# Operand sets of the down products: low parts written into the loaded tiles, loads and splits on other product numbers

## The chip, the cores and the metric

One core of a Trainium2 chip runs the whole program. The metric is device time in microseconds from launch to end, as the median of several runs. TensorE (PE) multiplies, VectorE (DVE) and ScalarE (ACT) work on tiles in the on-chip memory, GpSimd (POOL) and SyncE (SP) here mostly issue transfers (DMA).

## The reference, cut to what matters

Two layers of a hybrid encoder on 1024 positions of width 1024. Each layer ends in a gated feed-forward network of width 2816, which is where the change lies:

```python
for layer in range(DEPTH):
    ...
    hn2 = rmsnorm(h, norm2_g[layer])
    ff = jax.nn.silu(hn2 @ ffn_w_gate[layer]) * (hn2 @ ffn_w_up[layer])
    h = h + ff @ ffn_w_down[layer]
return rmsnorm(h, final_g)
```

All of it is float32.

## The kernel before

**Numbers in two parts.** Every operand of a matmul is split: a high part, cast by ACT to a rounded format (`...h`, `whi`, `whs`), and a low part, what is left, subtracted by DVE (`...l`, `wlo`, `wls`). A product of a 128 x 128 weight block and a 128 x 512 tile then takes three matmuls: high by high, high by low, low by high (L192, L193, L194 in `piece`).

**Quads.** Large parts of the feed-forward network are computed by a scheme of seven products in place of eight for a 2 x 2 block matrix. For it weights and activations are combined by additions first. A *gate quad* (`quad_items`) computes gate and up of one feature tile f from the normed activations (`rf`, `tt0` to `tt3`); a *down quad* (`down_quad`) computes two output tiles from a *chunk* of features. A product accumulates into the PSUM banks x, y, v and w (tiles `qx`, `qy`, `qv`, `qw`). The order of the seven is x with b11, y with t1, v with t0, x with b21, y with t2, w with t3, v with b22. Between them small operations run: `first` copies bank x into `qp` on ACT (L1325 in the down quads), `second` adds bank y to it as `qu` on DVE (L1329), `third` makes `qc` from y and v. In gate quads the results go through a tanh (`ts`, L1408 and L1425), then `half0` and `half1` (L1417 to L1430) form the feature tiles.

**Chunks.** Layer 0 has two chunks of down quads, of 8 and 6 features; layer 1 has three, of 8, 8 and 6. Four down quads belong to a chunk (two to the last one of a layer), so there are five *begins*, at which a new chunk's operands are needed for the first time. The first begin of a layer follows on the last gate quad. A product of a chunk of 8 features has 4 tiles and 12 matmuls, of one of 6 features 3 tiles and 9 matmuls.

**Operand sets.** When a feature pair is done, `keep` and `row` (L1215 to L1218, tiles `ft`) write the four blocks (b..) and the four combinations (t0 to t3) to DRAM (`fd`). At a begin the seven sets (`SETS`) come back: `op_load` issues one load per tile on SP's queue (L1225, into `fr`), `op_split` casts and subtracts (helper `split`, L115 and L116, into `foh` and `fol`). All these tiles, and most others of 128 x 512, come from one pool of 86 slots; an allocation waits until a slot is free.

**What sets the order.** The program is a list of items, one for each product with the small operations between. The table in `more` hangs loads and splits on product numbers: before the change set k of seven is loaded at product t0 - 12 + k * 17 // 10 and split at t0 - 4 + k, where t0 is the begin's number. (An eighth set, b12, of a layer's last chunk is loaded and split at numbers of its own, which stay.) A scheduler then puts the instructions of the list into an order for each engine, by priority in the list and by the time it believes operands and slots to be ready, so the order on an engine is not that of the list. Each engine works through its order strictly in sequence.

Weights come through SP's queue into four buffers (`raw`, L124), are combined (`sm`, `s`, L143 to L150) and split (L157 on ACT, L158 on DVE).

Of the kernel before, what the change touches and what calls it, by code (L numbers as in the profile page):

```python
# [8 lines left out]
F32 = mybir.dt.float32  # L9
F32R = mybir.dt.float32r  # L10
# [3 lines left out]
ADD, SUB, MUL = ALU.add, ALU.subtract, ALU.mult  # L14
# [13 lines left out]
QUAD_FROM = (8, 3)  # L28
DOWN_QUADS = 2
SETS = ("b11", "t1", "t0", "b21", "t2", "t3", "b22")  # L30
QUAD_LOOK = 5
NEG = -1e30
EPS = 1e-6
# [65 lines left out]
class Trunk:  # L99
# [99 lines left out]
    def emit(self):  # L199
# [11 lines left out]
        for i, (fn, gs) in enumerate(self.seq):  # L211
# [12 lines left out]
            if gs:  # L224
                n = max(pos[id(g)] for g in gs) + 1
                if isinstance(gs[0], QuadPart):
                    if self.split_ < min(len(order), n + QUAD_LOOK):
                        held = sum(last[id(g)] > i and not g.slots for g in order[:self.split_])
# [949 lines left out]
    def ffn_items(self, l, fill, head):  # L1178
# [3 lines left out]
        nc, V = self.nc, self.nc.vector  # L1182
        ff = [{}, {}]
        quads = QUAD_FROM[l]
        groups, chunks = GROUPS[l], CHUNKS[l]
# [4 lines left out]
        act, fd, ops = {}, {}, {}  # L1190
# [29 lines left out]
                put(c, f"t{k}", j, t)  # L1220

        def op_load(c, kind):
            ts = ops[c, kind] = [self.A("fr") for _ in range(chunks[c][1] // 2)]
            for j, t in enumerate(ts):
                nc.sync.dma_start(t, fd[c, kind, j])  # L1225

        def op_split(c, kind):
            ops[c, kind] = [self.split(t, "fo") for t in ops[c, kind]]

        def gate(f, h, g, st, part=None):  # L1230
            if part != 1:
# [225 lines left out]
        for i, (G, go, U, uo) in enumerate(blocks):  # L1457
            if i == 0:

                G1, go1, U1, uo1 = blocks[1]  # L1460
                a, b, c = (self.halves(x) for x in head[-3:])
# [27 lines left out]
        def at(t, fn):  # L1489
            more.setdefault(t, []).append((fn,))  # L1490

        for t0, c in begins:
            for k, kind in enumerate(SETS):
                at(t0 - 12 + k * 17 // 10, lambda c=c, kind=kind: op_load(c, kind))
                at(t0 - 4 + k, lambda c=c, kind=kind: op_split(c, kind))
        c = len(chunks) - 1
        end = 7 * len(made)

# [8 lines left out]
        at(end - 7 * DOWN_QUADS - 1, start_last)  # L1507
        at(end - 7 * DOWN_QUADS - 1, lambda: residual(H_AHEAD))
        at(end - 8, lambda: op_load(c, "b12"))
        at(end - 3, lambda: op_split(c, "b12"))  # L1510
        t = 0

# [25 lines left out]
        if fill:  # L1538
            a = len(head) + 12
            b = fill_end  # L1540
# [265 lines left out]
```

## Time and profile before

| | us |
|---|---|
| median of 3 runs | 2648.95 |
| lowest and highest | 2644.98, 2649.7 |
| the profiled execution's own time | 2647.83 |
| its span, first to last instruction | 2646.1 |
| TensorE busy in it | 2564.8 |

The 1.7 us between the profiled time and its span lie outside the instructions. Shares of busy time are means over stages with different limits: TensorE is busy almost always, so what counts is where it stands still, and which instruction ends that. The granted clock tells how fast TensorE ran in a stretch: 1.00 is 2.4 GHz, 0.50 is 1.2 GHz, values between are a mixture over time.

### The profile page before, as it was taken

How to read it: one execution, taken by the hardware profiler on the slowest of the kernel's cores; microseconds unless marked ns; L12 is line 12 of the kernel's file. 1: busy time of each engine (PE TensorE's matmuls, PEld its weight loads, DVE VectorE, ACT ScalarE, POOL GpSimd, SP SyncE). 2: the span in 40 equal slices, each digit the busy share in tenths (PEclk: the TensorE clock that was granted, in tenths of full speed). 3: DMA queues.
4: the chain of work that ended last, by engine and by line, in shares of the span. 5: the costliest groups of instructions: out<-in, count | busy, mean ns of one | idle time of the engine just before them, and what ended most of it. 6: DMA issues, size and time to landing. Idle time of an engine off the chain costs nothing.

```text
span 2646.1 us, 35134 instructions
## 1 busy us (share of the span) xinstructions
PE 2564.8 (97%) x12722; PEld 2088.1 (79%) x12722; DVE 1827.9 (69%) x3577; ACT 1022.1 (39%) x1949; POOL 321.3 (12%) x528
## 2 busy tenths in 40 slices
PE   8999899999999999998999999999999999998997
PEld 6787677887888888886787778888878888886776
DVE  9986878575977677677763465756377777676766
ACT  5336744422443333233444553453233222234432
POOL 0141011000142111011100001200001011111110
PEclk9999999999999999998999999999999999998998
DMA  3453435354174533255732244434322233255773
GB/s 139 136 186 118 136 120 180 124 186 140 55 197 132 98 110 108 96 202 137 200 133 76 72 140 161 159 120 167 127 92 93 102 104 116 92 199 156 176 190 123
DMA packets 160510, 357.01 MB, mean 135 GB/s; under 512 B 22048, under 2 KB 44832, under 8 KB 160336
## 3 DMA queue, kind: packets, MB, share of 16 engines
q1 hardware_dynamic: 117136, 236.28, 26.9%
q0 software_dynamic: 43200, 118.48, 15.9%
q8 instruction: 100, 1.64, 0.2%
q14 instruction: 74, 0.61, 0.1%
HBM read 230.97 MB, written 123.68 MB: 134 GB/s over the span
## 4 chain that ended last, share of the span: by engine, by line
PE 88%; DVE 7%; ACT 2%; issue 1%; DMA 1%; SPq 0%; DVEq 0%; ACTq 0%
PE pj L181 6%; PE pj L182 6%; PE pj L183 6%; PE qx L192 3%; PE qx L193 3%; PE qx L194 3%; PE qy L192 3%; PE qy L194 3%; PE qy L193 3%; PE qv L192 3%; PE qv L193 3%; PE qv L194 3%; PE wo L181 2%; PE wo L183 2%; PE wo L182 2%; PE br L181 2%
## 5 line engine op out<-in xcount | busy, mean ns | idle before, releaser
L181 PE MATMUL pj<-rah,whi 128*128 128x512 f32 x768 | 306.2, 399 | 0.4 <-DVE sm L804 0.4
L182 PE MATMUL pj<-ral,whi 128*128 128x512 f32 x768 | 300.1, 391 | 0.7 <-DVE ral L116 0.7
L183 PE MATMUL pj<-rah,wlo 128*128 128x512 f32 x768 | 299.9, 391 | 0.0
L170 DVE TENSOR_TENSOR wlo<-raw,whi 128x1024 fp32r<-128x1024 f32 (+1 forms) x126 | 145.7, 1156 | 168.3 <-ACT whi L169 159.0
L169 ACT CAST whi<-raw 128x1024 fp32r<-128x1024 f32 (+1 forms) x126 | 125.3, 995 | 273.9 <-PE pj L182 115.1
L181 PEld LDWEIGHTS pj<-rah,whi 128*128 128x128 f32 x768 | 144.7, 188 | 35.4 <-issue 4.7
L182 PEld LDWEIGHTS pj<-ral,whi 128*128 128x128 f32 x768 | 144.8, 189 | 30.9 <-DVE ral L116 2.6
L183 PEld LDWEIGHTS pj<-rah,wlo 128*128 128x128 f32 x768 | 144.5, 188 | 30.8
L1425 ACT ACTIVATE ts<-qu 128x512 f32<-128x512 f32 x33 | 20.9, 633 | 287.2 <-DVE qu L1423 287.2
L804 DVE CUSTOM_DVE_ANT_0 x<-s,bias,nsink 128x384 f32<-128x384 f32 (+1 forms) x128 | 67.5, 581 | 64.0 <-PE s L798 63.9
L1423 DVE TENSOR_TENSOR qu<-qu,qv 128x512 f32<-128x512 f32 x33 | 22.7, 687 | 125.8 <-PE qv L194 125.8
L192 PE MATMUL qx<-rfh,whi 128*128 128x512 f32 x264 | 102.7, 389 | 0.0
L193 PE MATMUL qx<-rfl,whi 128*128 128x512 f32 x264 | 102.7, 389 | 0.0
L194 PE MATMUL qx<-rfh,wlo 128*128 128x512 f32 x264 | 102.7, 389 | 0.0
L976 ACT COPY s5sg<-s5s 64x256 f32<-64x256 f32 x128 | 51.7, 404 | 128.8 <-DVE s5s L971 127.4
L181 PE MATMUL wo<-mgh,whi 128*128 128x512 f32 x256 | 100.0, 391 | 0.0
L1196 POOL DMA_DIRECT2D fd_b<-ts x60 | 32.6, 543 | 553.4 <-DVE ts L1419 464.2
L183 PE MATMUL wo<-mgh,wlo 128*128 128x512 f32 x256 | 99.7, 389 | 0.0
L182 PE MATMUL wo<-mgl,whi 128*128 128x512 f32 x256 | 99.6, 389 | 0.0
L157 ACT CAST whs<-s 128x512 fp32r<-128x512 f32 (+1 forms) x98 | 59.9, 612 | 99.3 <-DVE s L150 93.3
L157 ACT CAST whi<-sm 128x1024 fp32r<-128x1024 f32 (+1 forms) x49 | 50.6, 1033 | 122.7 <-PE qv L193 102.9
L158 DVE TENSOR_TENSOR wlo<-sm,whi 128x1024 fp32r<-128x1024 f32 (+1 forms) x49 | 58.9, 1202 | 41.8 <-ACT whi L157 41.7
(468 smaller groups left out, 7191.0 us busy)
## 6 DMA issues: line engine op xcount, KB each, us to landing
raw<-in_w_in SPq DMA_DIRECT2D x52, 512.0 KB
raw<-in_w_gate SPq DMA_DIRECT2D x44, 512.0 KB
raw<-in_w_up SPq DMA_DIRECT2D x44, 512.0 KB
fd_t<-ft POOLq DMA_DIRECT2D x72, 256.0 KB, 2.7
fr<-fd_t SPq DMA_DIRECT2D x72, 256.0 KB
g<-th POOLq DMA_DIRECT2D x64, 256.0 KB, 2.8
thr<-g SPq DMA_DIRECT2D x64, 256.0 KB
fd_b<-ts POOLq DMA_DIRECT2D x60, 256.0 KB, 2.3
```

The source lines that it names most:

```text
L157: nc.scalar.copy(g.hi[:, n], src)
L158: V.tensor_tensor(g.lo[:, n], src, g.hi[:, n].bitcast(F32), SUB)
L169: nc.scalar.copy(g.hi[:, :n], g.raw[:, :n])
L170: nc.vector.tensor_tensor(g.lo[:, :n], g.raw[:, :n], g.hi[:, :n].bitcast(F32), SUB)
L181: mm(ps, lhsT=wh, rhs=xh, start=k == 0, stop=False)
L182: mm(ps, lhsT=wh, rhs=xl, start=False, stop=False)
L183: mm(ps, lhsT=wl, rhs=xh, start=False, stop=k == n - 1)
L192: mm(ps, lhsT=wh, rhs=xh, start=start and k == 0, stop=False)
L193: mm(ps, lhsT=wh, rhs=xl, start=False, stop=False)
L194: mm(ps, lhsT=wl, rhs=xh, start=False, stop=k == len(xs) - 1)
L804: V.tensor_tensor_reduce(out=x[:, :n], in0=ps[:, :n], in1=self.bias[hd][:, bo:bo + n], op0=ADD, op1=ALU.min, scale=-1.0, scalar=self.nsink ...
L976: nc.scalar.copy(SG[64 * r:64 * r + 64, g * 256:(g + 1) * 256].rearrange("p (d n) -> p d n", d=2), Sv[64 * g:64 * g + 64, :, r])
```

## The change

The low part of a set is written into the tile that was loaded, so that a tile of a set holds two slots (loaded tile and high part) instead of three while it is split. And the product numbers of loads and splits are read from two tables, `LOADS` and `SPLITS`. Against the begin the loads of the seven sets move from -12, -11, -9, -7, -6, -4, -2 to -14, -10, -8, -7, -5, -4, -2, the splits from -4, -3, -2, -1, 0, 1, 2 to -10, -6, -4, -2, 0, 2, 3.

```diff
 SETS = ("b11", "t1", "t0", "b21", "t2", "t3", "b22")
+
+LOADS = (-14, -10, -8, -7, -5, -4, -2)
+SPLITS = (-10, -6, -4, -2, 0, 2, 3)
...
         def op_load(c, kind):
-            ts = ops[c, kind] = [self.A("fr") for _ in range(chunks[c][1] // 2)]
+            ts = ops[c, kind] = [self.A("fol", F32R) for _ in range(chunks[c][1] // 2)]
             for j, t in enumerate(ts):
-                nc.sync.dma_start(t, fd[c, kind, j])
+                nc.sync.dma_start(t.bitcast(F32), fd[c, kind, j])
 
         def op_split(c, kind):
-            ops[c, kind] = [self.split(t, "fo") for t in ops[c, kind]]
+
+            pairs = []
+            for lo in ops[c, kind]:
+                hi = self.A("foh", F32R)
+                nc.scalar.copy(hi, lo.bitcast(F32))
+                V.tensor_tensor(lo, lo.bitcast(F32), hi.bitcast(F32), SUB)
+                pairs.append((hi, lo))
+            ops[c, kind] = pairs
...
         for t0, c in begins:
-            for k, kind in enumerate(SETS):
-                at(t0 - 12 + k * 17 // 10, lambda c=c, kind=kind: op_load(c, kind))
-                at(t0 - 4 + k, lambda c=c, kind=kind: op_split(c, kind))
+            for kind, a, b in zip(SETS, LOADS, SPLITS):
+                at(t0 + a, lambda c=c, kind=kind: op_load(c, kind))
+                at(t0 + b, lambda c=c, kind=kind: op_split(c, kind))
```

The diff also moves line numbers: cast and subtraction of these sets are L1235 and L1236 in the changed kernel, the loads L1228, and lines behind them stand 10 further down (`first` L1335, `second` L1339), those ahead 3.

The number of instructions on each engine stays the same; their order does not. On DVE round the first begin of layer 0, before (`wlo` is the low part of the next down quad's combined weights, `qc` a sum of the last gate quad, `fol` low parts of the sets):

```order
L116 TENSOR_TENSOR fol<-fr,foh 128x512 x4
L1417 SCALAR_TENSOR_TENSOR ts<-ts,qx 128x512
L158 TENSOR_TENSOR wls<-raw,whs 128x512
L116 TENSOR_TENSOR fol<-fr,foh 128x512 x4
L158 TENSOR_TENSOR wlo<-sm,whi 128x1024
L1413 TENSOR_TENSOR qc<-qp,qv 128x512
L116 TENSOR_TENSOR fol<-fr,foh 128x512
L1418 TENSOR_TENSOR qp<-qp,qw 128x512
```

and now:

```order
L1427 SCALAR_TENSOR_TENSOR ts<-ts,qx 128x512
L161 TENSOR_TENSOR wls<-raw,whs 128x512
L1236 TENSOR_TENSOR fol<-fol,foh 128x512 x4
L1423 TENSOR_TENSOR qc<-qp,qv 128x512
L161 TENSOR_TENSOR wls<-s_11108,whs 128x512
L1428 TENSOR_TENSOR qp<-qp,qw 128x512
L1236 TENSOR_TENSOR fol<-fol,foh 128x512
L1429 SCALAR_TENSOR_TENSOR ts<-qp,ts 128x512
L1236 TENSOR_TENSOR fol<-fol,foh 128x512 x3
L1433 TENSOR_TENSOR qu<-qu,qv 128x512
L161 TENSOR_TENSOR wlo<-sm,whi 128x1024
```

`wlo`, which stood ahead of the gate's `qc`, stands behind `qc` and behind `qu`; the four `fol` of b21, which stood among the gate's sums, are all ahead of `qc`, and those of t2 ahead of `qu`.

A few instructions on, still DVE at that begin, before (the `ts` and `ft` are the last gate quad's `half1` and `row`; the first four `fol` are t2's, the second four t3's):

```order
L116 TENSOR_TENSOR fol<-fr,foh 128x512 x4
L1215 TENSOR_TENSOR ft<-ts 128x512
L1429 SCALAR_TENSOR_TENSOR ts<-ts,qu 128x512
L1430 SCALAR_TENSOR_TENSOR ts<-qc,ts 128x512
L1216 TENSOR_TENSOR ft<-ts,ft 128x512
L1217 TENSOR_TENSOR ft<-ts 128x512
L1218 TENSOR_TENSOR ft<-ts,ft 128x512
L116 TENSOR_TENSOR fol<-fr,foh 128x512 x4
L146 TENSOR_TENSOR s_11360<-raw,sm 128x512
```

and now (the first four `fol` are t3's, the last four b22's; `qu` is the first down quad's `second`):

```order
L1439 SCALAR_TENSOR_TENSOR ts<-ts,qu 128x512
L1218 TENSOR_TENSOR ft<-ts 128x512
L1440 SCALAR_TENSOR_TENSOR ts<-qc,ts 128x512
L1219 TENSOR_TENSOR ft<-ts,ft 128x512
L1220 TENSOR_TENSOR ft<-ts 128x512
L1221 TENSOR_TENSOR ft<-ts,ft 128x512
L149 TENSOR_TENSOR s_11324<-raw,sm 128x512
L1236 TENSOR_TENSOR fol<-fol,foh 128x512 x4
L1339 TENSOR_TENSOR qu<-qp,qy 128x512
L1236 TENSOR_TENSOR fol<-fol,foh 128x512 x4
```

t3's four still follow on `half1` and `row`; `second`, which stood further down behind b22's, stands between t3's and b22's.

On ACT round the second begin of layer 0 (`whi` from `sm` is the high part of combined weights, `qp` the copy of `first`), before; the first three `foh` are t1's, the next six t0's and b21's, the six behind `whi` t2's and t3's, the last three b22's:

```order
L115 CAST foh<-fr 128x512 x3
L1336 COPY dx<-qx 128x512
L157 CAST whs<-raw 128x384
L115 CAST foh<-fr 128x512 x6
L157 CAST whi<-sm 128x768
L157 CAST whs<-s_11808 128x384
L115 CAST foh<-fr 128x512 x6
L1325 COPY qp<-qx 128x512
L115 CAST foh<-fr 128x512 x3
```

and now (b21's, t2's, t3's and, behind `whi`, b22's):

```order
L1235 CAST foh<-fol 128x512 x3
L160 CAST whs<-s_11792 128x384
L1235 CAST foh<-fol 128x512 x3
L1335 COPY qp<-qx 128x512
L1235 CAST foh<-fol 128x512 x3
L160 CAST whi<-sm 128x768
L1235 CAST foh<-fol 128x512 x3
```

The casts of t2 and t3 and the copy, which stood behind `whi`, stand ahead of it.

## Rows read from the trace of the kernel before

**Rows 1.** The page, busy us (share of the span) xinstructions of each engine
```profile
PE 2564.8 (97%) x12722; PEld 2088.1 (79%) x12722; DVE 1827.9 (69%) x3577; ACT 1022.1 (39%) x1949; POOL 321.3 (12%) x528
```

**Rows 2.** Waits of PE: line, waited for: us in total, times, longest us
```profile
PE qw L193 <- DVE fol L116: 14.8, 5, 6.3
PE qw L192 <- ACT foh L115: 13.5, 5, 3.2
...
PE qv L192 <- DVE qc L1413: 5.5, 2, 2.8
```

**Rows 3.** Windows: stretch, its us, PE busy (xmatmuls), granted clock, DMA share, GB/s
```profile
1140.00:1200.00 60.00, 60.00 (x266) 1.00 0.56 194
1190.00:1250.00 60.00, 48.99 (x199) 0.89 0.47 122
1285.00:1315.00 30.00, 26.19 (x102) 0.89 0.74 203
...
2470.00:2510.00 40.00, 35.92 (x151) 0.96 0.64 134
2557.00:2587.00 30.00, 26.19 (x103) 0.89 0.65 186
```

**Rows 4.** Timeline of PE, layer 0's first begin: start, us, line, op [idle before]
```profile
1205.37 0.78 PE L192 MATMUL qv<-rfh,whs 128*128 128x512 f32 x1 [2.77 <-DVE qc L1413]
1205.95 0.63 PE L193 MATMUL qv<-rfl,whs 128*128 128x512 f32 x1
1206.38 0.63 PE L194 MATMUL qv<-rfh,wls 128*128 128x512 f32 x1
...
1218.84 0.79 PE L193 MATMUL qw<-fol,whs 128*128 128x512 f32 x1 [6.24 <-DVE fol L116]
```

**Rows 5.** Timeline of DVE at the same begin
```profile
1203.49 1.22 DVE L158 TENSOR_TENSOR wlo<-sm,whi 128x1024 fp32r<-128x1024 f32 x1 [2.29 <-ACT whi L157]
1204.63 0.68 DVE L1413 TENSOR_TENSOR qc<-qp,qv 128x512 f32<-128x512 f32 x1
...
1210.03 0.69 DVE L1423 TENSOR_TENSOR qu<-qu,qv 128x512 f32<-128x512 f32 x1 [1.71 <-PE qv L194]
...
1214.24 0.69 DVE L1215 TENSOR_TENSOR ft<-ts 128x512 f32<-128x512 f32 x1
...
1218.10 2.49 DVE L116 TENSOR_TENSOR fol<-fr,foh 128x512 fp32r<-128x512 f32 x4
```

**Rows 6.** Timeline of ACT, at layer 0's first begin and at its second
```profile
1210.81 0.63 ACT L1425 ACTIVATE ts<-qu 128x512 f32<-128x512 f32 x1 [2.66 <-DVE qu L1423]
...
1294.59 0.83 ACT L157 CAST whi<-sm 128x768 fp32r<-128x768 f32 x1 [7.87 <-issue]
...
1295.74 3.21 ACT L115 CAST foh<-fr 128x512 fp32r<-128x512 f32 x6
```

**Rows 7.** Timeline of PE, second begins of layer 0 and of layer 1
```profile
1297.96 0.80 PE L192 MATMUL qw<-foh,whs 128*128 128x512 f32 x1 [3.23 <-ACT foh L115]
1299.34 0.79 PE L193 MATMUL qw<-fol,whs 128*128 128x512 f32 x1 [0.58 <-DVE fol L116]
...
2487.39 0.50 PE L192 MATMUL qw<-foh,whs 128*128 128x512 f32 x1 [2.99 <-ACT foh L115]
2488.97 0.79 PE L193 MATMUL qw<-fol,whs 128*128 128x512 f32 x1 [1.09 <-DVE fol L116]
```

**Rows 8.** Two lines of DVE: op xcount, ns min/median/max, first and last start
```profile
L116 DVE TENSOR_TENSOR fol<-fr,foh x132: 681/686/693, 1185.0 to 2589.3; 128x512 fp32r<-128x512 f32 x132
...
L144 DVE TENSOR_TENSOR sm<-sm,raw x49: 557/691/698, 909.2 to 2550.3; 128x512 f32<-128x512 f32 x45, 128x384 f32<-128x384 f32 x4
```

**Rows 9.** Timeline of PE, a short idle in layer 0's gates
```profile
675.54 0.50 PE L181 MATMUL fg<-rfh,whi 128*128 128x512 f32 x1 [1.69 <-ACT rfh L115]
675.88 0.40 PE L181 MATMUL fu<-rfh,whi 128*128 128x512 f32 x1
```

**Rows 10.** Waits of SP's queue, 1140 to 1300
```profile
SPq L124 <- DVE s L150: 76.5, 6, 24.9
```

## The prediction

> **What bounds the kernel now.** I read the page's busy row first, then TensorE's waits, then its timeline at the places they name, then DVE's and ACT's timelines at the same places. TensorE is busy 2564.8 us, 97% of the span [rows 1], so a change in the operands' preparation is worth at most the time for which TensorE stands still on them, and what its clock loses after. The waits list names three such entries that belong to the chunk begins: on the low part `fol` 14.8 us, on the high part `foh` 13.5, on the gate's sum `qc` 5.5, together 33.8 us [rows 2]. The other entries of the list belong to code that the diff leaves alone.
>
> Idle time is not the whole loss. Behind a stall matmuls start 0.43 us apart (1205.95 to 1206.38), against 60 / 266 = 0.2256 us in an undisturbed stretch at granted clock 1.00 [rows 3, 4]. So I count the matmuls that are missing in a stretch round each begin [rows 3]. The first begin of layer 0 (1190 to 1250): 266 - 199 = 67, times 0.2256 = 15.1 us; layer 1's first begin has the same 199. The second begin of layer 0: 133 - 102 = 31, or 7.0 us. Layer 1's second: 177.3 - 151 = 26.3, or 5.9 us. Layer 1's third: 133 - 103 = 30, or 6.8 us. The sum, 2 x 15.1 + 7.0 + 5.9 + 6.8 = **49.9 us, is the ceiling** of what the change can bring: 33.8 idle and some 16 of slow clock.
>
> The Trainium skill, "TensorE: Matmul & The Clock Gate", section "Back-to-back issue gap", gives 512 / 2.4 + 2.5 = 216 ns for a warm matmul of 512 columns. By that pitch the ceiling would be an estimated 47.7 us. The trace's 0.2256 stays in the sum.
>
> **What happens at a begin.** Two patterns. (a) First begins. On DVE `wlo` stands ahead of `qc` and waits until 1203.49 for ACT, so `qc` comes at 1204.63 and the gate's seventh product starts 2.77 us late. Then DVE is full from 1210.03: `qu`, low parts of b21 and t2, the gate's six last sums (`half1` and `row`) from 1214.24 to 1218.10, and only then the four `fol` of t3, for which TensorE has been idle 6.24 us by 1218.84 [rows 4, 5]. (b) The other three begins. On ACT the cast `whi` takes a buffer that t0's product has to free first; it starts at 1294.59 after 7.87 us of idle, with the casts of t2 and t3 queued behind it. These run from 1295.74, and TensorE stands 3.23 + 0.58 us [rows 6, 7].
>
> **Part 1: low parts in the loaded tiles.** Nothing is added to an engine: one cast and one subtraction per tile as before, 132 of each. A subtraction in place costs what another does: `sm<-sm,raw` 691 ns, `fol<-fr,foh` 686 [rows 8]. The price is 0 +/- 132 x 0.005 us = 0.7 us of DVE time, hidden under TensorE either way. An operand tile holds two slots instead of three while it is split, so casts wait less for slots. I put that at 0 by itself; its effect is in the new order.
>
> **Part 2: loads and splits spread.** The same loads and splits, five begins of seven sets with three or four tiles each, move by up to six products of 12 x 0.2256 = 2.7 us (9 x 0.2256 = 2.0 us in the three-tile chunk).
>
> *`qc` at the first begins.* In the new order `wlo` stands behind `qc` and `qu`. In front of `qc` are the four subtractions of b21 instead (four take 2.49 us at 1218.10, so 0.60 apart). Counting DVE from the start s of the chunk's first product (s = 1194.28 in the trace), `qc` ends at about s + 5.9, and the gate's seventh product, now after eleven matmuls of t0, wants it at s + 7.9. The 2.77 us stall goes, with 2 us to spare.
>
> *t3 at the first begins.* Here the split of t3 still stands behind the gate's last sums: in the new order qu, wlo, ts, ft, ts, ft, ft, ft, s4, then t3's four. Moving t2 and b21 ahead has emptied the queue before `qu`, but not behind it. And a new wait is added: the sum `qu` of `second` (L1339) stands behind those four, and product t2 overwrites the bank that it reads. The chain from the end of the gate's seventh product (s + 10.8): `qu` 0.60, `wlo` 1.14 (its pitch from 1203.49 to 1204.63), six sums 3.86 (1214.24 to 1218.10), s4 0.60, four `fol` 2.4, `qu` 0.69 [rows 5] = 9.3; with 0.15 us of hand-over t2 starts at s + 20.25. Without stalls it would start at s + 13.6. So 6.65 us are still lost. Part of it shows as another new wait: b21's product waits for the copy of `first`, which stands on ACT behind the tanh (1210.81, 0.63 us, 0.78 after `qu`) [rows 6]: 0.60 + 0.18 + 0.63 after the seventh product's end and about 0.5 for the copy; that is 1.7 us of the 6.65, since only one matmul lies between. Behind both waits are queued, on TensorE, all matmuls of t2, t3 and b22, ready or not.
>
> The Trainium skill, "TensorE: Matmul & The Clock Gate", section "Step-by-step: what each phase is for", states that matmuls stay in program order and only weight loads are pulled ahead. The trace shows it: in the 6.24 us ahead of 1218.84 TensorE starts no matmul of any product [rows 4]. If it could step past a blocked product these 6.65 us would mostly vanish; that is rival A's time.
>
> On the clock: at layer 1's second begin 2.99 + 1.09 = 4.08 us of idle cost 5.9 in all, so 1.8 for the clock; at layer 0's second 3.81 idle cost 7.0, so 3.2 [rows 3, 7]. After 1.69 us of idle at 675.54 the next matmul came 0.34 us later, at no lasting drop [rows 9]. Of the new idle (1.7 and 4.9 us) only the second should drop the clock: I take 1.8, the shorter price, because the engine is busy on both sides of the short one. So a first begin loses 6.65 + 1.8 = 8.4 instead of 15.1: **6.7 us gained at each, 13.4 for two**; with 3.2 it is 10.6.
>
> *The other three begins.* In the new order t2's three casts and the copy stand ahead of `whi` on ACT (all of t3's too in the three-tile chunk of layer 0's second and layer 1's third begin; two of t3's four behind it in layer 1's second). TensorE no longer waits for them: t3's parts are there 3 us early. What comes last next is `qu` of `second` again: `whi` 0.83 [rows 6], `wlo` 1.14 x 768 / 1024 = 0.86, `qu` 0.69 after t0's product ends = 2.4 us, against twelve matmuls of b21 and t3 in between, 12 x 0.2256 = 2.7 us. The slack is **0.3 us** there, about 0.45 at layer 1's second. I take these stalls as gone: 7.0 + 5.9 + 6.8 = **19.7 us**.
>
> *Loads.* b11's loads go to SyncE's queue two products earlier, those of t1, t0 and t2 one later, and the splits move up: the lead from load to split, 8, 8, 7, 6, 6, 5, 4 products in the order of the sets, becomes 4, 4, 4, 5, 5, 6, 5. Its least, four products or 10.8 us, was there before for b22, and no wait on a load stands in TensorE's list. SyncE's own waits are on weights' buffers, up to 24.9 us [rows 10]; the loads' places among those are almost as before, so I put it at 0.
>
> **Sum.** 13.4 + 19.7 = 33.1 us. Profiled execution 2647.83 - 33.1 = 2614.7. The median lies 1.1 higher: **2615.8**, say 2616.
>
> **Rivals.** *A, all goes:* the last sums of the gate get out of t3's way and nothing replaces them: 2648.95 - 49.9 = 2599. For it: all splits start earlier. Against it: t3's stand behind the same sums, and the waits are the same kind. *B, the thin slacks fail:* 0.3 us is a fraction of one DVE operation (0.60), and if one comes in between at the three later begins, a stall of one to three us with its clock takes most of the 19.7: only 13.4 is left, 2635.5. *C, the change doesn't do what it says at the first begins:* the earlier splits only shift DVE's backlog, and 15.1 stays at both: 2648.95 - 19.7 = 2629. *D, slower: late loads.* Place: SyncE's queue ahead of a begin, where loads follow a weight load that waits (24.9 us at worst [rows 10]). With the lead cut to 10.8 us for three sets a late load holds ACT and DVE, which take their work in order, and with them the gates' `qc`. Price: each us late passes on, plus 1.8 us of clock. At five begins it turns the sign from 33.1 / 5 - 1.8 = 4.8 us late at each; 10 us late at each gives 2615.8 + 5 x 11.8 = 2675. Against it: b22 lived with that lead before.
>
> **Chances.** Forecast (2606 to 2626, with partial failures) 0.58; A 0.08; B 0.17; C 0.07; D 0.10, half of it deep enough to be slower, half to land within 0.2% (5.3 us, about what a measurement of this kernel can tell from no change). Faster 0.90, same 0.05, slower 0.05. Range 2600 to 2638: from just above A past B, leaving out A and D.
>
> **What would show it.** In the profile after: no wait of the seventh product on `qc`; at the two first begins one idle of about 1.7 us before qx ended by the copy or tanh, and one near 5 us before qy ended by `qu`; at the three others no wait over 0.5 us; 227 to 232 matmuls in the 60 us round a first begin; the three entries' 33.8 us of idle down to about 13, and the other entries as before. Wrong it would be made by waits on `foh` or `fol` behind a load, or by a wait of qy t2 at the later begins.

## The result, and the profile after

The changed kernel takes **2614.23 us** (median of 4 runs, 2614.16 to 2614.47) against 2649.32 for the kernel before, run beside it (2644.98 to 2650.9). The ratio is 0.987, 95% interval 0.9853 to 0.9887: some 35 us gained. The profiled execution's span fell from 2646.1 to 2612.7.

TensorE's waits of the changed kernel (line, waited for: us in total, times, longest us). The first and the last are all that is left at the begins; the one between them belongs to the program's start.

```profile
PE qy L195 <- DVE qu L1339: 8.6, 2, 4.3
PE pj L184 <- ACT xgh L372: 7.0, 1, 7.0
...
PE qx L195 <- ACT qp L1335: 3.4, 2, 1.7
```

The three entries of [rows 2] on `fol`, `foh` and `qc`, 33.8 us, are gone. Two new ones of 12.0 us stand there, each twice: once at the first begin of each layer. Windows of the same kernel (stretch, its us, PE busy (xmatmuls), granted clock, DMA share, GB/s):

```profile
1190.00:1250.00 60.00, 54.00 (x230) 0.97 0.57 140
...
1260.00:1300.00 40.00, 40.00 (x178) 1.00 0.86 242
2360.00:2420.00 60.00, 54.00 (x227) 0.94 0.58 158
2440.00:2490.00 50.00, 50.00 (x222) 1.00 0.78 190
2530.00:2570.00 40.00, 40.00 (x178) 1.00 0.62 183
```

At the first begins 36 and 39 matmuls are missing, 8.1 and 8.8 us by the 0.2256 us apart, where 67 were [rows 3]. At layer 0's second begin (1260 to 1300) and layer 1's second and third (2440 to 2490, 2530 to 2570) none is. So 49.9 us of loss became 16.9: 33.0 us, which is the fall of the span but for 0.4.

TensorE at layer 0's first begin, after (start, us, line, op, idle before):

```profile
1194.13 0.39 PE L195 MATMUL qx<-foh,whi 128*128 128x512 f32 x1
...
1206.86 0.50 PE L195 MATMUL qx<-foh,whi 128*128 128x512 f32 x1 [1.69 <-ACT qp L1335]
1207.20 0.39 PE L196 MATMUL qx<-fol,whi 128*128 128x512 f32 x1
...
1214.20 0.71 PE L195 MATMUL qy<-foh,whs 128*128 128x512 f32 x1 [4.31 <-DVE qu L1339]
1214.71 0.63 PE L196 MATMUL qy<-fol,whs 128*128 128x512 f32 x1
1215.14 0.63 PE L197 MATMUL qy<-foh,wls 128*128 128x512 f32 x1
...
1217.95 0.39 PE L195 MATMUL qy<-foh,whs 128*128 128x512 f32 x1
```

b21's product waits 1.69 us for the copy of `first`, t2's product 4.31 us for the sum of `second`; only behind the second wait are matmuls 0.43 us apart. DVE in that time:

```profile
1199.48 0.69 DVE L1423 TENSOR_TENSOR qc<-qp,qv 128x512 f32<-128x512 f32 x1
...
1204.98 0.69 DVE L1433 TENSOR_TENSOR qu<-qu,qv 128x512 f32<-128x512 f32 x1 [0.60 <-PE qv L197]
1205.59 1.22 DVE L161 TENSOR_TENSOR wlo<-sm,whi 128x1024 fp32r<-128x1024 f32 x1
1206.72 0.68 DVE L1439 SCALAR_TENSOR_TENSOR ts<-ts,qu 128x512 f32<-128x512 f32 x1
...
1210.46 0.68 DVE L149 TENSOR_TENSOR s<-raw,sm 128x512 f32<-128x512 f32 x1
1211.06 2.49 DVE L1236 TENSOR_TENSOR fol<-fol,foh 128x512 fp32r<-128x512 f32 x4
1213.47 0.68 DVE L1339 TENSOR_TENSOR qu<-qp,qy 128x512 f32<-128x512 f32 x1
```

`qc` comes at 1199.48, where before it stood behind `wlo` [rows 5]. From the gate's `qu` at 1204.98 on DVE does not pause until `second`'s `qu` ends at 1214.15, and TensorE goes on 0.05 us later.

### The profile page after: what moved, and what is told of

Read it like the earlier page. It is cut to its first block, busy times and chain, and to the rows that moved or that the text cites. A ratio compares the mean times of both kernels' runs of the same rounds, so it can differ in the third digit from the quotient of the medians.

```text
span 2612.7 us, 35123 instructions
## 1 busy us (share of the span) xinstructions
PE 2550.7 (98%) x12722; PEld 2079.1 (80%) x12722; DVE 1826.8 (70%) x3577; ACT 1022.5 (39%) x1949; POOL 322.5 (12%) x528
## 4 chain that ended last, share of the span: by engine, by line
PE 88%; DVE 8%; ACT 2%; issue 1%; DMA 1%; SPq 0%; DVEq 0%; ACTq 0%
PE pj L184 6%; PE pj L185 6%; PE pj L186 6%; PE qy L195 3%; PE qy L196 3%; PE qy L197 3%; PE qv L195 3%; PE qv L196 3%; PE qv L197 3%; PE qx L195 3%; PE qx L197 3%; PE qx L196 3%; PE wo L184 2%; PE wo L186 2%; PE wo L185 2%; PE br L184 2%
## 5 line engine op out<-in xcount | busy, mean ns | idle before, releaser
L1236 DVE TENSOR_TENSOR fol<-fol,foh 128x512 fp32r<-128x512 f32 x132 | 83.3, 686 | 0.2 <-ACT foh L1235 0.2
```

The source lines that it names most:

```text
L1236: V.tensor_tensor(lo, lo.bitcast(F32), hi.bitcast(F32), SUB)
```

## The experiments

**The two halves of the change, each alone.** The first experiment (e1) keeps the in-place low parts and puts the old numbers back:

```diff
-LOADS = (-14, -10, -8, -7, -5, -4, -2)
-SPLITS = (-10, -6, -4, -2, 0, 2, 3)
+LOADS = (-12, -11, -9, -7, -6, -4, -2)
+SPLITS = (-4, -3, -2, -1, 0, 1, 2)
```

> Low parts in the loaded tiles, but loads and splits at the old product numbers. Theory 1 (the gain is in the new numbers; the slots are worth nothing by themselves, as the prediction put it): about 2649, the three stalls of before still there. Theory 2 (fewer slots held while a set is split already changes the order on DVE and ACT): in the new order wlo stands behind the gate's qc and, at the second begins, whi behind the casts of t2 and t3, so the qc stall (5.5 us) and the 19.7 us of the three later begins go; t3's products still stand ahead of b21's on TensorE and wait for t3's low parts behind the gate's last sums, about 6 us idle at each first begin, 10 us with the clock. Time about 2649 - 19.7 - 2 x 5 = 2619.

Measured: 2620.92 us (2619.92 to 2621.04), ratio 0.9894 (0.9879 to 0.9908). Its waits on the begins' operands:

```profile
PE qw L195 <- ACT foh L1235: 8.3, 2, 4.1
PE qw L196 <- DVE fol L1236: 7.3, 2, 3.8
```

The wait on `qc` and those of the three later begins are gone; what is left are two stalls of t3's products at each first begin, 7.8 us of idle (theory 2 said about 6, and named the low parts alone; half of it is for the high parts). So theory 2 holds but for that: the in-place half alone brings 27.8 us, where the prediction put it at 0 by itself. TensorE at the two first begins (columns as above, here and below):

```profile
1190.00:1250.00 60.00, 52.06 (x222) 0.94 0.54 147
...
2365.00:2425.00 60.00, 52.35 (x220) 0.91 0.54 146
```

The second one (e2) keeps the new numbers and gives the low part a fresh tile again:

```diff
-            ts = ops[c, kind] = [self.A("fol", F32R) for _ in range(chunks[c][1] // 2)]
+            ts = ops[c, kind] = [self.A("fr") for _ in range(chunks[c][1] // 2)]
...
-                nc.sync.dma_start(t.bitcast(F32), fd[c, kind, j])
+                nc.sync.dma_start(t, fd[c, kind, j])
...
-            pairs = []
-            for lo in ops[c, kind]:
-                hi = self.A("foh", F32R)
-                nc.scalar.copy(hi, lo.bitcast(F32))
-                V.tensor_tensor(lo, lo.bitcast(F32), hi.bitcast(F32), SUB)
-                pairs.append((hi, lo))
-            ops[c, kind] = pairs
+            ops[c, kind] = [self.split(t, "fo") for t in ops[c, kind]]
```

> New product numbers for loads and splits, but three slots per tile while it is split. Theory 1 (the numbers carry the gain): about 2614, as the changed kernel. Theory 2 (both matter): the casts of t2 stand ahead of whi at the later begins, so most of 19.7 us goes, but at the first begins wlo stands ahead of qc again, so 2.8 us of idle on qc at each come back beside the chain to second's qu: about 2614 + 2 x 4 = 2622.

Measured: 2634.10 us (2632.21 to 2636.36), ratio 0.9945 (0.993 to 0.9959). The waits:

```profile
PE qv L195 <- DVE qc L1417: 9.3, 2, 4.6
PE qx L195 <- ACT qp L1329: 5.9, 4, 1.9
PE qy L195 <- DVE qu L1333: 5.3, 2, 2.7
PE qw L196 <- DVE fol L119: 1.3, 3, 0.8
```

Theory 1 falls. Theory 2 named the waits on `qc` and on `second`'s `qu`, but its size is wrong by 12 us. The waits for the copy (`qp`), 1.9 us at each first begin, are not in it, `qc` costs 4.6 us in place of 2.8, and round layer 1's second begin 3.4 us of idle are left, in short waits on `qp` and `fol`:

```profile
1190.00:1250.00 60.00, 50.80 (x201) 0.91 0.49 132
...
2365.00:2425.00 60.00, 50.78 (x197) 0.89 0.51 149
...
2440.00:2490.00 50.00, 46.63 (x201) 1.00 0.81 215
```

DVE at the first begin of this kernel shows why `qc` is even later than before:

```profile
1203.87 1.23 DVE L161 TENSOR_TENSOR wlo<-sm,whi 128x1024 fp32r<-128x1024 f32 x1 [2.33 <-ACT whi L160]
1205.01 1.89 DVE L119 TENSOR_TENSOR fol<-fr,foh 128x512 fp32r<-128x512 f32 x3
1206.82 0.68 DVE L1417 TENSOR_TENSOR qc<-qp,qv 128x512 f32<-128x512 f32 x1
```

`wlo` stands ahead of `qc` again and waits for ACT, and now three of b21's low parts, which the new numbers moved forward, stand between the two: 4.6 us of idle instead of 2.8. Numbers alone are worth 14.6 us, in place alone 27.8, both 34.5 to 35, so 7 to 8 us are in either half. The missing matmuls say where. At the first begins the numbers alone bring nothing (65 and 69 missing, 67 before), in place alone brings some 10 us (44 and 46), and the numbers on top of it another 3 to 4 (36 and 39). At the three later begins the numbers alone remove all but 21 missing matmuls (4.7 us, at layer 1's second), in place alone all: what the halves share lies there.

**The two tables, each alone**, with the low parts in place. Split numbers new, load numbers old (e5):

```diff
-LOADS = (-14, -10, -8, -7, -5, -4, -2)
+LOADS = (-12, -11, -9, -7, -6, -4, -2)
```

> In place, the new split numbers, the old load numbers. Theory (of the two tables only the splits' matters, since no wait on a load shows before or after): the order at the begins is nearly that of the changed kernel, 4.3 + 1.7 us idle at each first begin, none at the others: 2612 to 2617. Rival (b11's set needs its earlier load, its lead would be two products instead of four): a wait on foh or fol of b11 at the begins, 2 to 5 us at each, 2625 to 2640.

Measured: 2616.26 us (2615.73 to 2619.16), ratio 0.9884 (0.987 to 0.9899). No wait on a load, so the rival falls. The waits have shifted, though: more before b21's product, less before t2's:

```profile
PE qx L195 <- ACT qp L1335: 8.5, 2, 4.2
...
PE qy L195 <- DVE qu L1339: 4.6, 2, 2.7
```

Load numbers new, split numbers old (e8):

```diff
-SPLITS = (-10, -6, -4, -2, 0, 2, 3)
+SPLITS = (-4, -3, -2, -1, 0, 1, 2)
```

> In place, the new load numbers, the old split numbers. Theory (only the splits' table matters): as e1, 2619 to 2623, with the waits of t3's products on foh and fol at the first begins. Rival (earlier loads let the scheduler place the splits earlier as well): 2612 to 2617.

Measured: 2617.22 us (2616.22 to 2618.43), ratio 0.9884 (0.9868 to 0.9901). The time lies 0.2 us above the rival's range, and 1.8 below the theory's; the waits are the kind that the theory said, t3's products on `foh` and `fol`:

```profile
PE qw L196 <- DVE fol L1236: 7.6, 2, 3.8
...
PE qw L195 <- ACT foh L1235: 5.8, 2, 2.9
```

Neither is shown cleanly: against e1 the wait on `foh` is 1.26 us shorter at each first begin, where the scheduler put seven of t0's matmuls behind the gate's seventh product. Either table alone, on top of the in-place low parts, is worth some 3 to 4 us, and both together 7, each taken against the kernel before run beside it.

**Is it the number of slots?** The in-place half was meant here as two slots per tile instead of three. Here (e7) is e1 with ten slots fewer in the pool:

```diff
-N_SLOTS = 86
+N_SLOTS = 76
```

> e1 (in place, old numbers) with a pool of 76 slots instead of 86. Theory S (e1 gains because slots come free sooner on the chip): with ten slots fewer the waits for slots come back, 2625 to 2649. Theory O (e1 gains because the order on DVE and ACT round the begins is another, which it still is at 76 slots): as e1, 2619 to 2624.

Measured: 2630.88 us (2629.49 to 2632.74), ratio 0.9938 (0.9923 to 0.9953), 10 us above e1. The number lies in theory S's range, the place mostly does not: the idle at the two first begins rose from 15.6 to 16.4 us, and some 2.4 us came back at the later ones (on `qc`, and 0.8 of `fol`); one wait of 3.3 us stands in the attention part, and the rest is spread.

```profile
PE qw L195 <- ACT foh L1235: 9.4, 2, 4.7
PE qw L196 <- DVE fol L1236: 7.8, 3, 3.5
...
PE qv L195 <- DVE qc L1352: 1.6, 3, 0.7
```

So slots are worth something all over the program, but 17 of e1's 28 us remain, and the stalls of the three later begins do not return when they are short. What removed these is the order: with 76 slots ACT still has `whi` behind the casts of t2 and t3 at layer 0's second begin. Orders that were built but not run point the same way. With three tiles per operand, pools of 84 and 87 slots give the order of before, 80 moves one operation, and 76 moves a few, none of them where the first begins and layer 0's second stall. In place, an unused third tile leaves the new order as it is. So the write into the loaded tile gives the scheduler another order, and the size of the pool, between 76 and 87 slots, does not. Why it does so was not settled.

**What is left at the first begins.** The prediction named DVE's chain to `second`'s `qu`. The next kernel (e3) moves the last gate quad's `half1` (with its `row`) behind the first down quad's `second` in the list:

```diff
             do(p[2])
             main.append(e[1])
+            main.extend(late)
+            late = []
...
-            main.extend(e[5:])
+            if i + 1 == begins[0][0] // 7:
+                main.append(e[5])
+                late = e[6:]
+            else:
+                main.extend(e[5:])
```

> The changed kernel with the last gate quad's half1 (and its row) moved behind the first down quad's second in the program. Theory R (what is left at the first begins is DVE's chain to second's qu, in which half1 and row take 3.9 us): the idle of 4.3 us before qy at the first begins goes, the 1.7 us before qx stays, TensorE's clock does not fall there; 2614.2 - 2 x (4.3 + 2) = about 2601. Rival (something else, as late loads or t2's operands, holds t2's product as well): less than 3 us.

Measured: 2602.53 us (2600.54 to 2603.92), ratio 0.9827 (0.981 to 0.9843). One wait is left at the begins:

```profile
PE qx L195 <- ACT qp L1335: 3.4, 2, 1.7
```

and the clock no longer falls in the window of 1190 to 1250 (columns as above):

```profile
1190.00:1250.00 60.00, 58.31 (x257) 1.00 0.60 160
```

The one after it (e4) also moves `gate1` (the gate's `qu` and its tanh) behind the down quad's copy:

```diff
             main.append(e[0])
+            main.extend(soon)
+            soon = []
...
-                main.append(e[5])
+                soon = [e[5]]
```

> As the run before, and the last gate quad's gate1 (sum and tanh) also moved behind the first down quad's first (the copy). Theory R: the copy comes ahead of the tanh on ACT, so the 1.7 us before qx go too: 2601 - 2 x 1.7 = about 2598, no wait over 0.5 us on the five begins' operands. Rival: the new order of TensorE (t3's products pulled ahead of t2's) waits for t3's low parts instead: 2 x 1 to 2 x 3 us more.

Measured: 2600.04 us (2599.95 to 2600.28), ratio 0.9816 (0.9801 to 0.983). The wait for the copy is gone. A wait of t3's products stands in its place, as the rival said, but for the high parts and not the low ones, 1.43 us twice:

```profile
PE qw L195 <- ACT foh L1235: 2.9, 2, 1.4
```

ACT has t3's casts behind the tanh and a weight cast there, so in the last kernel (e6) their split goes one product earlier, on top of e4:

```diff
-SPLITS = (-10, -6, -4, -2, 0, 2, 3)
+SPLITS = (-10, -6, -4, -2, 0, 1, 3)
```

> As e4 (gate1 and half1 late), and t3's split at product 1 in place of 2 after the begin. Theory R: the last 1.4 us before qw at each first begin are ACT's casts of t3, which stand behind the tanh and two weight casts there; now they stand ahead of the copy, so no wait on the five begins' operands is left: 2600.0 - 2 x 1.4 = 2597.2. Rival: t3's four subtractions, now ahead of the gate's qu on DVE, bring a wait on qu or qp of 1 to 2 us at each first begin: 2600 to 2602.

Measured: **2597.62 us** (2596.52 to 2599.51), ratio 0.9812 (0.9798 to 0.9827). It is the lowest median of all here, though against the kernel before run beside each (2647.73 here, 2648.74 for e4) e6 gains only 1.4 us more than e4, which the times alone do not settle. The waits do: no wait on a begin's operands or sums is left in TensorE's list, and the stretches round the begins are as full as any:

```profile
1190.00:1250.00 60.00, 60.00 (x266) 1.00 0.65 163
2360.00:2420.00 60.00, 60.00 (x267) 1.00 0.73 194
1265.00:1305.00 40.00, 40.00 (x178) 1.00 0.76 228
```

DVE does the gate's last sums a little later there, and nobody waits for them:

```profile
1207.15 0.69 DVE L1433 TENSOR_TENSOR qu<-qu,qv 128x512 f32<-128x512 f32 x1
1207.75 1.22 DVE L161 TENSOR_TENSOR wlo<-sm,whi 128x1024 fp32r<-128x1024 f32 x1
1208.89 0.69 DVE L149 TENSOR_TENSOR s<-raw,sm 128x512 f32<-128x512 f32 x1
1209.49 0.68 DVE L1339 TENSOR_TENSOR qu<-qp,qy 128x512 f32<-128x512 f32 x1
```

Between the gate's `qu` and `second`'s stand two operations now, where eight and t3's four low parts stood; those four run ahead of the gate's `qu`.

## Why the prediction was right

**The ceiling of 49.9 us** was right. Counting missing matmuls instead of idle time gave 2648.95 - 49.9 = 2599; the kernel with no stall left at any begin (e6) took 2597.62, 50.1 us less than the kernel before run beside it.

**The new waits at the first begins** were right in place, order and size. The wait on the copy was forecast at 1.7 us and is 1.69. The one on `second` was forecast at 4.9 and is 4.31. The chain came to 9.3 + 0.15 us; it ran from 1204.98 to 1214.20, 9.22. The chunk's first product starts at 1194.13, the prediction's s, so t2 starts at s + 20.07, where s + 20.25 was forecast: late by 6.5 us against s + 13.6, where 6.65 was forecast. Of these only 6.0 are idle. The rest, and most of the 0.6 us between 4.9 and 4.31, lies at the short wait, whose cost is a little more than its idle: b21's matmuls behind it start up to 0.34 us apart at first, and e3, with the 1.69 us alone, misses 9 matmuls, 2.0 us. That half1 and `row` are the part of the chain that matters is shown by e3: without them in the chain the 4.31 us go, at both begins.

**The clock** was sized about right. From t2's first matmul on, nine matmuls at layer 0's first begin took 3.75 us (1214.20 to 1217.95) where 2.0 would do at full clock, and twelve at layer 1's took 4.96 where 2.7 would do:

```profile
2387.37 0.80 PE L195 MATMUL qy<-foh,whs 128*128 128x512 f32 x1 [4.31 <-DVE qu L1339]
...
2392.33 0.40 PE L195 MATMUL qw<-foh,whs 128*128 128x512 f32 x1
```

That is 1.7 and 2.2 us more, where 1.8 was taken out of 1.8 to 3.2. With the 6.5 us by which t2 is late this makes 8.2 and 8.7, the 8.1 and 8.8 counted; 8.4 was forecast. That the short wait costs no clock is shown by e3: with the 1.69 us alone the granted clock of the window is 1.00.

**The three later begins** were right. The slack there was forecast at 0.3 us. ACT of the changed kernel at layer 0's second begin, then DVE, then TensorE:

```profile
1287.31 0.84 ACT L160 CAST whi<-sm 128x768 fp32r<-128x768 f32 x1 [4.43 <-PE qv L196]
```

```profile
1288.18 0.96 DVE L161 TENSOR_TENSOR wlo<-sm,whi 128x768 fp32r<-128x768 f32 x1 [1.76 <-ACT whi L160]
1289.06 0.68 DVE L1339 TENSOR_TENSOR qu<-qp,qy 128x512 f32<-128x512 f32 x1
```

```profile
1290.06 0.39 PE L195 MATMUL qy<-foh,whs 128*128 128x512 f32 x1
```

`qu` ends at 1289.74 and t2's product starts at 1290.06: 0.32 us to spare. At layer 1's third begin it is 0.32 us again, and at its second 0.40 (0.45 was forecast), with two of t3's subtractions in the chain between `wlo` and `qu`, as the prediction had read in the order. So the thin slack held at all three, and rival B fell. `whi` waits for t0's product, as the prediction said of the kernel before (where [rows 6] name no releaser), but the casts that TensorE needs are ahead of it.

**`qc`** was right: it ends at 1200.17 and the gate's seventh product takes it at about 1202.06 (the first of its twelve matmuls), 1.9 us to spare where 2 were forecast.

**Wrong was the share of the parts.** "I put that at 0 by itself; its effect is in the new order" had the second half right, but the working then booked the new order wholly under part 2. e1 and e2 show that the in-place low parts alone make 27.8 of the 35 us, and the numbers alone 14.6. The sum was right because it was read from the built order of the whole change, where both are in.

**Rivals.** A did not come (2599), but e6 shows what it needed: the last gate quad's sums out of the way. C fell: the backlog left at each first begin costs 8.1 to 8.8, not 15.1. D fell: no wait on a load appears at the begins, not even in e5 with b11's lead cut to two products. The Trainium skill's statement on TensorE's sequence ("TensorE: Matmul & The Clock Gate", "Step-by-step: what each phase is for") agrees with the trace after: for the 4.31 us ahead of 1214.20 no matmul starts, and with t2's product late t3's follows only behind it.

## What to carry to other kernels

Before an operand is prepared earlier, see what else stands in the same engine's sequence: here the longest stall came from the sums of the work that was ending, and moving those behind the first sum that the next work needs gave another 15 to 17 us with the same instructions (e6, one split a product earlier included; 15.0 by the gains against the kernel before, 16.6 by the medians). Count the matmuls that are missing in a stretch, not the idle time alone: here 33.8 us of idle stood for 49.9 us, since behind the long waits matmuls started 0.43 us apart. Where a scheduler decides the order, the change of one tile can move as much as a table of numbers; so read the built order, and take the parts of a change one at a time before crediting either.

## What was not expected of the hardware

An idle of 1.4 to 1.7 us (e4 and e3) left the granted clock of the window at 1.00, while the 4.31 us in the changed kernel lowered it at both first begins. The 4.31 us follow on 1.69 us of idle there, but the single 2.77 us of the kernel before did the same: behind them matmuls start 0.43 us apart [rows 4]. In e2, 3.4 us in several short waits round layer 1's second begin left the clock at 1.00 (2440 to 2490) and still cost 21 matmuls, 4.7 us. Not of the chip, but not expected either: 76 instead of 86 slots cost 10 us (e7 against e1), spread over the program.
